# Loads of the delta-rule chain in a function of their own, issued two tiles ahead into three buffers

## The chip, the cores and the metric

The kernel runs on 1 core of one Trainium2 chip. The metric is the time of one execution on the device in microseconds (us), taken as the median of several runs. The core's engines each work through a queue of their own, in order: TensorE (PE, matmuls), VectorE (DVE), ScalarE (ACT), GpSimd (POOL) and SyncE (SP), which here issues nearly all DMA transfers.

## The reference

Two layers (DEPTH = 2) of a hybrid block on 2048 latent tokens and a prefix of 256 context tokens. Each layer projects the normalised input once and feeds three groups of heads, whose outputs are concatenated and projected back: a bidirectional state-space scan (SSD), a bidirectional gated delta rule (GDN), and attention over all 2304 tokens. The change concerns the delta rule. Per direction, head and chunk of 64 tokens it computes

```python
def step(S, inp):
    qd, kd, u_i, w_i, a_i, d_i = inp
    v_new = u_i - jnp.einsum('bhcd,bhde->bhce', w_i, S)
    o = jnp.einsum('bhcd,bhde->bhce', qd, S) + jnp.einsum('bhij,bhje->bhie', a_i, v_new)
    S = S * d_i[..., None, None] + jnp.einsum('bhcd,bhce->bhde', kd, v_new)
    return S, o
```

so each chunk needs the state S that the chunk before it leaves.

## The kernel before

The tokens are 18 tiles of 128 (NT = 18, 2 of context and 16 latent). In each layer the kernel projects the input, prepares the delta rule (`gdn_pre`, `gdn_solve`, which store per tile what the chain needs in DRAM), runs the SSD, and then the delta-rule chain (`gdn_chain`) beside attention; at the end comes the output projection (line 1231).

Attention is written as a generator. Eight of its 24 large units stand before the chain in the code, the others behind it. A planner of the framework turns the code into one queue per engine ahead of time: it gives an instruction a place when it expects its inputs to be there and its buffers to be free, by its own estimates of durations, and prefers what stands earlier in the code. So attention's matmuls (lines 531, 562, 563, 556) fill PE between those of the chain, and with them come attention's maxima (`mx`, line 533, and `nm`, line 535) and the low halves `pl` (line 571) on VectorE and the exponentials on ScalarE. Once planned, the queues run in that order on the chip.

In the chain, tile u stands for tile u of the forward direction and tile rev(u) of the backward one, side by side. Three functions work on it, all in pool `gw` with two buffers per name, and `slot` gives them banks of one PSUM pool of four; buffers and banks of a pool are handed out in the order of the code.

- `prep(u)` (line 1036) issues 13 DMA loads on SP's queue: `acv` (3 pieces by `by_chunk`, so its rows carry line 1034), `xf` (4, line 1050), `xt_` (2, line 1052), `kq` (2, line 1054, shown as `kqc`) and `er` (2, line 1055). Then it computes: `kq` times `er` in place (line 1056 on VectorE for k, line 1060 on GpSimd for q), `kdw` (line 1058, GpSimd), the mask on `acv` in place (line 1061, VectorE), and the off-diagonal block of the inverse by two rounds of small matmuls (lines 1067 and 1076) with copies on ScalarE. After it `er` and `xt_` are no longer needed; `kq`, `acv` and `xf` are read on by the step.
- `step(u)` does two chunks (s = 0, 1), each a chain of k S (line 1100), r (line 1104, VectorE), the inverse times r (line 1114), V (line 1119, ScalarE), the update (line 1123; the output at lines 1109 and 1125) and the new S (`Sc`, line 1127, VectorE).
- `out(u)` normalises and gates the output of the tile, in the second half of the tiles.

The loop calls prep(u + 1), then step(u), then out(u - 1). The tiles `xf` are kept by hand in a list of two, `xf[u % 2]`, as parts of them stay zero.

Of the kernel before, what the change touches and what calls it, by code (L numbers as in the profile page):

```python
# [9 lines left out]
F32 = mybir.dt.float32  # L10
# [7 lines left out]
P = 128  # L18
# [4 lines left out]
NT = NTOK // P  # L23
# [14 lines left out]
def rev(t):  # L38
    return TC - 1 - t if t < TC else NT + TC - 1 - t
# [45 lines left out]
def hybrid_kernel(ctx, tc, x, c, ctx_in, c_ctx, norm_w, w_mod, b_mod, w_in, conv_w, conv_b, ssd_A_log,  # L85
# [158 lines left out]
    for l in range(DEPTH):  # L244
# [246 lines left out]
        with ExitStack() as bx:  # L491
# [13 lines left out]
            def slot(name):  # L505
                return psg[1].tile([P, 512], F32, name=name, tag="g")
# [108 lines left out]
            def next_layer():  # L615
                if not last:
                    Ln.append(layer_tiles())
                    layer_vectors(l + 1, Ln[0], ps=sslot)
                    yield
                    yield from modulation(l + 1, Ln[0], ps=sslot, wmp=wmp)  # L620
                    layer_rows(l + 1, Ln[0])
# [59 lines left out]
            ot0 = TC if last else 0  # L681
# [324 lines left out]
            def gdn_chain(rq):  # L1006
# [6 lines left out]
                with ExitStack() as gx:  # L1013
                    gr = gx.enter_context(tc.tile_pool(reuse_waits="tile", name="gr2", bufs=1))
                    gw = gx.enter_context(tc.tile_pool(reuse_waits="tile", name="gw2", bufs=2))
                    xf = [gr.tile([P, 2, 4, 64], F32, name=f"xf{i}") for i in range(2)]
                    for i in range(2):
                        nc.gpsimd.memset(xf[i], 0.0)
                    S = gw.tile([P, 4, 64], F32, name="Sc")
                    nc.gpsimd.memset(S, 0.0)  # L1020
# [8 lines left out]
                    def by_chunk(d, dram2, tile3, store=False):  # L1029
                        v = dram2.rearrange("(c p) x -> p c x", c=2)  # L1030
                        for i in ((slice(0, 2),) if d == 0 else (0, 1)):
                            j = i if d == 0 else 1 - i
                            a, b_ = tile3[tk[d], i], v[:, j]
                            nc.sync.dma_start(b_, a) if store else nc.sync.dma_start(a, b_)

                    def prep(u):
                        tl = (u, rev(u))
                        want_o = u >= ot0
                        xu = xf[u % 2]
                        xt = gw.tile([P, 2, 4, 32], F32, name="xt_")  # L1040
                        kq = gw.tile([P, 2, 4, P], F32, name="kqc")
                        er = gw.tile([P, 4, P], F32, name="er")
                        acv = gw.tile([P, 2, 4, 4, 64], F32, name="acv")
                        k0 = 0 if want_o else 1
                        for d in range(2):
                            td = tl[d]
                            tsl = slice(td * P, (td + 1) * P)
                            by_chunk(d, pre_d[td, :, k0:4].rearrange("p k h n -> p (k h n)"), acv[:, :, k0:4].rearrange("p c k h n -> p c (k h n)"))
                            for a, bb, cx in ((d, b0, c0), (1 - d, b1, c1)):
                                nc.sync.dma_start(xu[bb[d], :, :, cx[d]].rearrange("p c h i -> p (c h) i"),  # L1050
                                                  xd_d[d, 0, td, a].rearrange("c h j i -> j (c h) i"))
                            nc.sync.dma_start(xt[b0[d]].rearrange("p c h i -> p (c h) i"), xd_d[d, 1, td, d].rearrange("c h j i -> j (c h) i"))
                            nk = 2 if want_o else 1
                            nc.sync.dma_start(kq[dk[d], 0:nk].rearrange("p k h n -> p (k h) n"), kt_d[0:nk * 256, tsl].rearrange("(h p) n -> p h n", p=64))
                            nc.sync.dma_start(er[dk[d]], eg_d[d:d + 1, :, u].to_broadcast([64, 4, P]))
                        nc.vector.tensor_tensor(out=kq[:, 0], in0=kq[:, 0], in1=er, op=ALU.mult)
                        kdw = gw.tile([P, 2, 4, 64], F32, name="kdw")
                        nc.gpsimd.tensor_tensor(out=kdw, in0=acv[:, :, 3], in1=kdc[:, u, :, :, None].to_broadcast([P, 2, 4, 64]), op=ALU.mult)
                        if want_o:
                            nc.gpsimd.tensor_tensor(out=kq[:, 1], in0=kq[:, 1], in1=er, op=ALU.mult)  # L1060
                            nc.vector.tensor_tensor(out=acv[:, :, 0], in0=acv[:, :, 0], in1=msk[:, None, None, :].to_broadcast([P, 2, 4, 64]), op=ALU.mult)
                        pv = slot("pv")
                        pvv = pv[:, 0:256].rearrange("p (c h n) -> p c h n", c=2, h=4)
                        for c in range(2):
                            for h in range(4):
                                for d in range(2):
                                    nc.tensor.matmul(pvv[b1[d], c, h, :], acv[b0[d], 1 - c if d else c, 1, h, c1[d]], xt[b0[d], c, h, :],
                                                     start=True, stop=True, tile_position=(b0[d].start, b1[d].start))
                        vt = gw.tile([P, 2, 4, 32], F32, name="vt")
                        for d in range(2):  # L1070
                            nc.scalar.activation(out=vt[b1[d]], in_=pvv[b1[d]], func=AF.Copy, scale=-1.0)
                        pzv = pv[:, 256:512].rearrange("p (c h n) -> p c h n", c=2, h=4)
                        for c in range(2):
                            for h in range(4):
                                for d in range(2):
                                    nc.tensor.matmul(pzv[b0[d], c, h, :], vt[b1[d], c, h, :], xu[b1[d], c, h, c1[d]],
                                                     start=True, stop=True, tile_position=(b1[d].start, b0[d].start))
                        for d in range(2):
                            nc.scalar.copy(out=xu[b0[d], :, :, c1[d]], in_=pzv[b0[d]])
                        return xu, kq, acv, kdw  # L1080
# [84 lines left out]
                                nc.sync.dma_start(mx_d[384:640, n0:n0 + 64].rearrange("(m p) n -> p m n", p=P), mt[:, c, :, tk[d]])  # L1165

                    pend = None
                    nxt = prep(0)
                    for u in range(NT):
                        cur, nxt = nxt, prep(u + 1) if u + 1 < NT else None  # L1170
                        S, ox = step(u, S, *cur)
                        if pend is not None:
                            out(*pend)
                        pend = (u, *ox) if ox is not None else None
# [14 lines left out]
            for _ in range(8):  # L1189
                next(att)  # L1190
            banks(0, 4)
            gdn_chain(rq)
            for _ in att:
                pass
# [55 lines left out]
            pend, ahead = [], next_layer()  # L1250
# [53 lines left out]
```

## Time and profile before

| what | value |
|---|---|
| median of 3 runs | 4039.15 us (4035.92 to 4040.36) |
| the profiled execution | 4035.59 us |
| its span | 4033.8 us |
| mean granted clock of PE | 0.969 |
| PE busy | 3776.4 us (94%) |
| VectorE busy | 2720.7 us (67%) |
| ScalarE busy | 1800.4 us (45%) |
| GpSimd busy | 1351.1 us (33%) |

The profile is of one execution; times inside it are counted from the start of its span. A row of a wait names who waited, for whom, the us in total, how often, and the longest. In a timeline row the bracket at the end is the idle time of the engine just before the instruction, and what ended it. PE's clock is given as the granted share of full speed: 1.00 is 2.4 GHz and 0.50 is 1.2 GHz, and a value between them is a mean over a stretch.

### The profile page before, as it was taken

What the parts mean: (1) busy time and instruction counts of PE and PEld (TensorE: products, weight loads), DVE (VectorE), ACT (ScalarE), POOL (GpSimd) and SP (SyncE); (2) the same over time, 40 slices, a digit from 0 to 9 for tenths busy, and PEclk for the clock granted to TensorE, in tenths of its full rate; (3) what the DMA queues carried; (4) which work ended last, traced back from release to release, by engine and by line L of the source; (5) the groups of instructions that cost most, each with busy time, mean ns of one, the idle gap of its engine ahead of it and who ended that gap; (6) DMA issues with size and microseconds to landing.
All of it is one profiled execution on the core that took longest, in us unless ns stands there. A gap on an engine that the chain in (4) does not pass through costs nothing. (4 is left out here: it accounts for less than half of the span.)

```text
span 4033.8 us, 70483 instructions
## 1 busy us (share of the span) xinstructions
PE 3776.4 (94%) x25750; PEld 2839.4 (70%) x25750; DVE 2720.7 (67%) x5372; ACT 1800.4 (45%) x3728; POOL 1351.1 (33%) x1760
## 2 busy tenths in 40 slices
PE   7999999999999888897999999999898999888989
PEld 5899999554566556565678999996554665556667
DVE  6556573789977567774547574746888776667733
ACT  5343332443466455564214443423333655556610
POOL 5112130477476221321213030303774662123100
PEclk9999999999999889998999999999999999989999
DMA  6343432345222544535744433332452215444344
GB/s 202 98 144 112 133 105 95 104 151 173 69 60 60 111 105 103 116 73 181 241 153 130 152 111 130 118 100 77 144 175 72 61 55 118 101 104 120 85 140 154
DMA packets 549798, 477.72 MB, mean 118 GB/s; under 512 B 133128, under 2 KB 487372, under 8 KB 549452
## 3 DMA queue, kind: packets, MB, share of 16 engines
q1 hardware_dynamic: 507596, 437.82, 37.1%
q10 hardware_dynamic: 41856, 35.40, 2.9%
q8 instruction: 203, 3.33, 0.3%
q14 instruction: 143, 1.17, 0.1%
HBM read 328.91 MB, written 144.18 MB: 117 GB/s over the span
## 5 line engine op out<-in xcount | busy, mean ns | idle before, releaser
L565 ACT ACTIVATE pe<-pst 128x512 f32<-128x512 f32 (+1 forms) x876 | 511.8, 594 | 692.0 <-PE pst L563 654.3
L533 DVE TENSOR_REDUCE mx<-pq 128x1 f32<-128x512 f32 (+1 forms) x972 | 590.6, 626 | 131.1 <-PE pq L531 127.0
L531 PE MATMUL pq<-khh,q 128*128 128x512 f32 (+1 forms) x972 | 459.9, 498 | 38.7 <-DVE mx L533 32.1
L556 PE MATMUL po<-pe,v 128*65 128x512 f32 x960 | 488.5, 597 | 0.8 <-ACT os__11676 L579 0.8
L562 PE MATMUL pst<-q,khh 128*128 128x512 f32 (+1 forms) x876 | 429.3, 490 | 16.8 <-DVE mx L533 14.0
L455 PE MATMUL ps<-lo,wh 128*128 128x384 f32 (+2 forms) x1296 | 441.3, 340 | 0.0
L455 PE MATMUL ps<-hi,wl 128*128 128x384 f32 (+2 forms) x1296 | 441.0, 340 | 0.0
L455 PE MATMUL ps<-hi,wh 128*128 128x384 f32 (+2 forms) x1296 | 440.9, 340 | 0.0
L571 DVE TENSOR_TENSOR pl<-pe,ph 128x512 fp32r<-128x512 f32 x396 | 309.6, 786 | 118.6 <-ACT ph L570 54.3
L563 PE MATMUL pst<-qm,klo 65*128 65x512 f32 (+1 forms) x876 | 356.9, 408 | 0.0
L401 PE MATMUL ps<-wh,hi 128*128 128x320 f32 (+1 forms) x1120 | 354.4, 318 | 0.1
L401 PE MATMUL ps<-wl,hi 128*128 128x320 f32 (+1 forms) x1120 | 350.8, 314 | 0.0
L401 PE MATMUL ps<-wh,lo 128*128 128x320 f32 (+1 forms) x1120 | 350.2, 315 | 0.5 <-DVE lo L366 0.5
L531 PEld LDWEIGHTS pq<-khh,q 128*128 128x128 f32 x972 | 186.7, 195 | 190.2 <-DVE mx L533 73.6
L570 ACT CAST ph<-pe 128x512 fp32r<-128x512 f32 x396 | 243.8, 620 | 94.0 <-PE po L556 36.4
L376 DVE TENSOR_TENSOR wl<-wt,wh 128x1024 fp32r<-128x1024 f32 (+3 forms) x144 | 175.3, 1246 | 160.2 <-ACT wh L375 159.8
L556 PE MATMUL po<-ph,vh 128*65 128x512 f32 x792 | 262.2, 413 | 7.7 <-ACT os__20088 L579 4.6
L562 PEld LDWEIGHTS pst<-q,khh 128*128 128x128 f32 x876 | 171.3, 196 | 128.7 <-issue 53.5
L455 PEld LDWEIGHTS ps<-lo,wh 128*128 128x128 f32 x1296 | 244.0, 188 | 10.8 <-issue 0.4
L455 PEld LDWEIGHTS ps<-hi,wh 128*128 128x128 f32 x1296 | 243.5, 188 | 10.3
L455 PEld LDWEIGHTS ps<-hi,wl 128*128 128x128 f32 x1296 | 243.4, 188 | 10.3
L1231 PE MATMUL psd<-woh,mh 128*128 128x512 f32 x544 | 218.7, 402 | 19.0 <-ACT mh L1222 17.6
(588 smaller groups left out, 8136.4 us busy)
## 6 DMA issues: line engine op xcount, KB each, us to landing
wt<-in_w_in_dram SPq DMA_DIRECT2D x72, 512.0 KB
wmt<-in_w_mod_dram SPq DMA_DIRECT2D x48, 512.0 KB
pre_d<-pre SPq DMA_DIRECT2D x34, 512.0 KB
acv<-pre_d SPq DMA_DIRECT2D x34, 512.0 KB
kqc<-kt_d SPq DMA_DIRECT2D x68, 256.0 KB
acv<-pre_d SPq DMA_DIRECT2D x68, 256.0 KB
wt<-in_w_in_dram SPq DMA_DIRECT2D x24, 668.0 KB
wt<-in_w_in_dram SPq DMA_DIRECT2D x24, 640.0 KB
```

What stands on the lines that cost most here:

```text
L376: nc.vector.tensor_tensor(out=wl[:, ks, :], in0=wt, in1=wh[:, ks, :].bitcast(F32), op=ALU.subtract)
L401: nc.tensor.matmul(ps, hh[:, k, a], ww[:, k, :], start=(n == 0), stop=(n == 3 * KD - 1))
L455: nc.tensor.matmul(ps, ww[:, k, m * P:(m + 1) * P], hh[:, k, s0:s0 + sn], start=(n == 0), stop=(n == 3 * KD - 1))
L531: nc.tensor.matmul(pq[:, :n], q2[:, u * P:(u + 1) * P], khh[:, kvh, k0t * P + a:k0t * P + a + n], start=True, stop=True)
L533: nc.vector.tensor_reduce(mx[:, i:i + 1], pq[:, :n], axis=AX.X, op=ALU.max)
L556: nc.tensor.matmul(po[0:65, :qn], v[:, kt, vs], p[:, :qn], start=(kt == k0t and j == 0), stop=(kt == k1t - 1 and j == len(ops) - 1))
L562: nc.tensor.matmul(pt[:, :qn], khh[:, kvh, ks], q2[:, :qn], start=True, stop=False)
L563: nc.tensor.matmul(pt[:, :qn], klo[:, kvh, ks], qm[:, :qn], start=False, stop=True)
L565: nc.scalar.activation(out=pe[:, :qn], in_=pt[:, :qn], func=AF.Exp, scale=0.125)
L570: nc.scalar.copy(out=ph, in_=pe)
L571: nc.vector.tensor_tensor(out=pl, in0=pe, in1=ph.bitcast(F32), op=ALU.subtract)
L1231: nc.tensor.matmul(ps, a, w[k][:, n * 512:n * 512 + 512], start=(k == 0 and i == 0), stop=(k == KD - 1 and i == 2))
```

## The change

`prep` is split. A function `load(u)` allocates the five tiles and issues the 13 loads; `prep` takes the tiles and only computes. The five tiles get three buffers in place of two: `xf` becomes a list of three with `xf[u % 3]`, the others get `bufs=3`. The loop issues load(0) and load(1) before prep(0), and load(u + 2) ahead of prep(u + 1). The transfers, the arithmetic, `step` and `out` stay.

```diff
-                    xf = [gr.tile([P, 2, 4, 64], F32, name=f"xf{i}") for i in range(2)]
-                    for i in range(2):
+                    xf = [gr.tile([P, 2, 4, 64], F32, name=f"xf{i}") for i in range(3)]
+                    for i in range(3):
                         nc.gpsimd.memset(xf[i], 0.0)
...
-                    def prep(u):
+                    def load(u):
                         tl = (u, rev(u))
                         want_o = u >= ot0
-                        xu = xf[u % 2]
-                        xt = gw.tile([P, 2, 4, 32], F32, name="xt_")
-                        kq = gw.tile([P, 2, 4, P], F32, name="kqc")
-                        er = gw.tile([P, 4, P], F32, name="er")
-                        acv = gw.tile([P, 2, 4, 4, 64], F32, name="acv")
+                        xu = xf[u % 3]
+                        xt = gw.tile([P, 2, 4, 32], F32, name="xt_", bufs=3)
+                        kq = gw.tile([P, 2, 4, P], F32, name="kqc", bufs=3)
+                        er = gw.tile([P, 4, P], F32, name="er", bufs=3)
+                        acv = gw.tile([P, 2, 4, 4, 64], F32, name="acv", bufs=3)
                         k0 = 0 if want_o else 1
...
                             nc.sync.dma_start(er[dk[d]], eg_d[d:d + 1, :, u].to_broadcast([64, 4, P]))
+                        return u, xu, xt, kq, er, acv
+
+                    def prep(u, xu, xt, kq, er, acv):
+                        want_o = u >= ot0
                         nc.vector.tensor_tensor(out=kq[:, 0], in0=kq[:, 0], in1=er, op=ALU.mult)
...
                     pend = None
-                    nxt = prep(0)
+                    ahead = [load(0), load(1)]
+                    nxt = prep(*ahead.pop(0))
                     for u in range(NT):
-                        cur, nxt = nxt, prep(u + 1) if u + 1 < NT else None
+                        if u + 2 < NT:
+                            ahead.append(load(u + 2))
+                        cur, nxt = nxt, prep(*ahead.pop(0)) if ahead else None
                         S, ox = step(u, S, *cur)
```

## Rows read from the trace of the kernel before

**Rows 1.** The page's first part: busy us, share of the span, instructions.

```profile
PE 3776.4 (94%) x25750; PEld 2839.4 (70%) x25750; DVE 2720.7 (67%) x5372; ACT 1800.4 (45%) x3728; POOL 1351.1 (33%) x1760
```

**Rows 2.** Table by stages: the stretches with the chain, layers 0 and 1.

```profile
core 0: us, PE busy (x) PEld busy (x) DVE busy (x) ACT busy (x) POOL busy (x), PEclk, DMA share, GB/s
...
1326.00:1822.00 496.00, 435.02 (x5307) 293.65 (x5306) 343.21 (x617) 290.58 (x557) 119.86 (x109) 0.91 0.46 105
...
3336.00:3808.00 472.00, 420.62 (x5161) 283.00 (x5160) 335.89 (x606) 285.76 (x545) 115.14 (x102) 0.94 0.45 108
```

**Rows 3.** The same table: the chain's end in layer 1, after its last loads.

```profile
3755.00:3790.00 35.00, 34.90 (x357) 23.34 (x353) 29.82 (x61) 25.96 (x48) 8.98 (x7) 1.00 0.14 36
```

**Rows 4.** Waits of PE in the two stretches, layer 0, then layer 1.

```profile
engine line waited for: us in total, times, longest us
PE pv L1067 <- DMA acv<-pre_d: 22.6, 9, 4.8
PE po L556 <- DVE pl L571: 8.3, 6, 3.1
...
PE pq L531 <- DVE nm L535: 2.5, 1, 2.5
PE pv L1067 <- DMA xt__12789<-xd_d: 1.2, 1, 1.2
...
PE pv L1067 <- DMA acv<-pre_d: 23.7, 10, 5.0
PE pq L531 <- DVE mx L533: 6.3, 4, 2.2
...
PE p L1100 <- DVE Sc L1127: 0.8, 1, 0.8
...
PE pv L1067 <- DMA xt__33913<-xd_d: 0.3, 1, 0.3
```

**Rows 5.** Timeline of VectorE: one tile, and S before the last step.

```profile
start us, us, engine line op out<-in xcount [idle before <-releaser]
3510.38 0.41 DVE L1127 TENSOR_TENSOR Sc<-sd,p 128x256 f32<-128x256 f32 x1
...
3514.56 0.69 DVE L1056 TENSOR_TENSOR kqc<-kqc,er 128x512 f32<-128x512 f32 x1 [2.27 <-DMA kqc<-kt_d]
...
3772.33 0.41 DVE L1127 TENSOR_TENSOR Sc<-sd,p 128x256 f32<-128x256 f32 x1
```

**Rows 6.** Timeline of PE at the same places.

```profile
3517.30 0.22 PE L1067 MATMUL pv<-xt__35007,acv 32*32 32x32 f32 x2 [3.56 <-DMA acv<-pre_d]
3517.45 0.68 PE L1100 MATMUL p<-Sc,kqc 64*64 64x64 f32 x16
...
3772.80 0.68 PE L1100 MATMUL p<-Sc,kqc 64*64 64x64 f32 x16
```

**Rows 7.** Timeline of SP's queue in the same tile: DMA issues.

```profile
3507.67 0.61 SPq L1054 DMA_DIRECT2D kqc<-kt_d  x1
...
3511.18 1.15 SPq L1034 DMA_DIRECT2D acv<-pre_d  x1
...
3516.40 1.26 SPq L1055 DMA_DIRECT2D er<-eg_d  x2
3523.04 0.80 SPq L1052 DMA_DIRECT2D xt__35343<-xd_d  x2
```

**Rows 8.** View of tile Sc: count, duration, first and last start of line 1127.

```profile
L1127 DVE TENSOR_TENSOR Sc<-sd,p x72: 404/418/424, 1357.7 to 3779.9; 128x256 f32<-128x256 f32 x72
```

**Rows 9.** What line 1056 waited for (us, times); then line 1061, layer 0.

```profile
  DMA kqc<-kt_d: 66.7, 26
...
  DMA er<-eg_d: 1.9, 3
...
DVE acv L1061 <- DMA acv<-pre_d: 6.3, 4, 2.2
```

**Rows 10.** Timeline of a tile where VectorE alone stopped PE.

```profile
3415.37 0.69 DVE L1056 TENSOR_TENSOR kqc<-kqc,er 128x512 f32<-128x512 f32 x1 [2.09 <-DMA kqc<-kt_d]
...
3417.79 0.45 PE L556 MATMUL po<-pl,vh 128*65 128x512 f32 x1 [3.02 <-DVE pl L571]
```

**Rows 11.** Table by stages, 5 us each, at and after the wait.

```profile
3515.00:3520.00 5.00, 2.70 (x28) 2.23 (x29) 5.00 (x9) 0.62 (x1) 1.37 (x1) 0.88 0.93 235
3520.00:3525.00 5.00, 5.00 (x70) 2.88 (x69) 2.16 (x5) 3.32 (x7) 1.21 (x1) 0.78 0.10 18
```

## Prediction

> **What bounds the kernel now.** I read the page first: TensorE (PE) is busy 94% of a span of 4033.8 us [rows 1], so a gain has to come out of the 6% in which it is idle, or out of time in which it is busy at the lower clock. The table by stages says where that is. In the two stretches that hold the delta-rule chain (1326 to 1822 us in layer 0, 3336 to 3808 us in layer 1) PE is busy 435.0 of 496 us and 420.6 of 472 us, with a mean granted clock of 0.91 and 0.94 [rows 2]. That is 61.0 + 51.4 = 112.4 us idle. What PE ran below full pace I take as busy time x (1 - clock): 435.0 x 0.09 + 420.6 x 0.06 = 39 + 25 = 64 us. Where the chain's last loads have landed (3755 to 3790 us), PE is busy 34.90 of 35 us at clock 1.00 [rows 3], so attention can fill PE around the chain.
>
> Next the waits of PE in these stretches [rows 4]. Line 1067, the first matmuls of the preparation, waited 38.5 us in layer 0 (five rows, the first and last shown) and 34.0 us in layer 1 (six rows), mostly for the load of `acv`: 72.5 us. Waits for VectorE (DVE) take 17.7 us (four rows, 10 waits) and 13.2 us (four rows, 9 waits): 30.9 us in 19 waits, 1.6 us each. The other 9.0 us belong to ScalarE at the stage's end and to gaps too short for the view.
>
> One tile in detail. The state S is done at 3510.38 + 0.41 = 3510.8 us [rows 5]. Next on PE's queue stands line 1067, which waits 3.56 us for `acv`, until 3517.30; line 1100, which needs S and nothing of `acv` but takes its PSUM bank after line 1067's, runs right behind it at 3517.45, 6.7 us after its input was there [rows 6]. In the last step, where no preparation is pending, line 1100 follows S by 3772.80 - 3772.74 = 0.06 us [rows 5, 6]. So the load stands in the chain and, PE's queue being in order, in front of attention too. SP's queue says why: the loads of `kq` and `acv` go out at 3507.67 and 3511.18, as the step that used their buffers ends, while `er` and `xt_`, whose buffers come free inside the preparation, go out at 3516.40 and 3523.04 for the tile after the next [rows 7]. The order of the code does not hold the loads back; two buffers do.
>
> **The change, part by part.** It adds no transfer: the 13 DMA issues of a tile stay, on SP's queue. It adds one memset of `xf` per layer (on GpSimd, ahead of the chain, beside attention: nothing) and 17 KiB per partition (`xf` 2, `xt_` 1, `kq` 4, `er` 2, `acv` 8). The larger pool may reach into the space where w_out is staged and hold that back until the chain ends; the last S comes at 3779.9 us [rows 8], 28 us before the stretch ends at 3808, and will come earlier, so I cost it at nothing; without this cover I would put it at the size of the 9 us that stand at the stage's end now.
>
> *Line 1067.* Tile u+2's loads go out when step u-1 ends and are used a whole step later. A tile takes up to 26 us (472 us over 18 tiles [rows 2]); `acv` landed 6.1 us after its issue (3511.18 to 3517.30) [rows 6, 7]. 26 against 6 leaves no wait: the 72.5 us go, but for some 5 us of the first tile. What SP is moved past are the partial-sum loads and stores and attention's q loads; they are used a step later and have slack. Banks are handed out in the order of the code, so `pv` of tile u+1 gets its bank after the last of step u-1; it is then ready, and I take no new wait there (bounds: none, or the 0.68 us of line 1100's matmuls a tile [rows 6]).
>
> *What is late next: VectorE.* Line 1056 multiplies `kq` in place by `er`. It needs no new buffer, so nothing holds it until its turn: the planner will put it into VectorE's queue where it expects `kq` to have landed, now in the middle of the step before. On the chip `kq` lands later than that: 2.27 us idle in this tile [rows 5], 79.2 us over the kernel (four rows, 33 waits), 2.2 us a tile [rows 9]. Everything on VectorE waits behind it, attention's `pl` and `mx`, and then PE. In the tile at 3415 us this alone stopped PE for 3.02 us, with VectorE idle 2.09 us [rows 10]. Today this wait mostly lies under that of line 1067 and costs little of its own; the cover goes. The bounds are 0 (the chain's own matmuls, which are no longer late, fill PE) and 36 x 3.02 = 109 us; I take the mean of the waits for VectorE that are seen, 36 x 1.6 = 58 us, since PE gets about 1 us of chain work to run meanwhile.
>
> Here a rule of the Trainium skill speaks against the change (DMA: Bandwidth & Descriptors, Rules for kernel authors): to hide a DMA, issue it early and wait for it late. The early issue is what the diff does; line 1056 still waits early (2.27 us [rows 5]), so by this rule the time would be that of the second rival, 4015 us, and not the sum below.
>
> *The clock.* After this wait the granted clock is 0.78 over 3520 to 3525 us [rows 11]: part of the time at the 1.2 GHz level. I let the 64 us shrink with the idle time (bounds 0 and 64).
>
> **The sum**, against the profiled execution's 4035.6 us (its span 4033.8; the median of the three runs is 3.5 us higher, inside their spread): idle 72.5 + 30.9 - 58 = 45 us; clock 64 x 45 / 103.4 = 28 us. 4035.6 - 73 = 3963 us. The chain itself becomes shorter by more (about 5 us a tile, 90 us a layer), but its end does not set the time: attention's matmuls behind it do, and they are all still there.
>
> **Rivals.** *Both waits vanish.* For it: the chain's end at 99.7% busy [rows 3], and that line 1056 gets a whole step of slack if the planner leaves it next to line 1067. Against: nothing in the code makes it wait for that. 103 us idle and most of the 64 us of clock go: 4036 - 156 = 3880 us (3870 to 3915). The Trainium skill's reading of a repeated gap as too few buffers (Perfetto Trace Analysis, Optimization Strategy) gives this outcome; the tile at 3415 us, stopped by VectorE alone, shows that buffers are not all of it.
>
> *The wait only moves.* Line 1056 stops PE for 2.2 us a tile, VectorE's full wait, or more: 36 x 2.2 = 79 us stay of 103, 24 us idle and 64 x 24 / 103 = 15 us of clock are saved, 3996 us; at 2.9 us a tile (103.4 / 36, today's mean) nothing is saved. 3996 to 4036, I say 4015 us. For it: rows 10. The case in which the third buffers bring no load forward lies at its upper end.
>
> *Slower: two waits on VectorE.* `acv` lands 2.7 us after `kq` is usable (3517.30 against 3514.56). If line 1061, the mask on `acv`, is put at its expected landing too, VectorE waits a second time, 2.7 - 0.7 (line 1056's work) = 2.0 us. So far that wait is small (6.3 us in 4 waits in layer 0 [rows 9]), as PE's stop delays what stands in front of it. Then 36 x (2.2 + 2.0) = 151 us idle against 103, and 64 x 48 / 103 = 30 us more of clock: up to 4114 us, I say 4080. It decides from the point where PE loses more than 2.9 us a tile. Against: the planner's distance from line 1056 to 1061 covers most of it today.
>
> **How the numbers follow.** Forecast (3930 to 3996) 0.47, both vanish 0.18, only moved 0.22, slower 0.13. The range 3890 to 4045 leaves out half of the first rival and most of the last, 2 in 10. A measurement can tell 0.2%, 8 us, from no change. Faster by more than that: 0.47 + 0.18 + 0.14 of the second rival = 0.79; the same: its other 0.08 and 0.01 of the last; slower 0.12.
>
> **What will show it.** Right: line 1067 no longer among PE's long waits for `acv`; line 1100 follows S within 3 us in every step (6.7 us in the tile above); the last S (now 3779.9 us [rows 8]) comes some 100 us or more earlier; PE's rest is ended by `pl`, `mx` and `nm`, with line 1056 still waiting some 2 us a tile for `kq`. Wrong, towards 3880: line 1056 without a wait and clock 1.00 throughout. Wrong, upwards: line 1067 still waits, or lines 1056 and 1061 wait over 3 us together and PE with them.

## The result, and the profile after

The changed kernel takes 4000.9 us in the median of four runs (3989.3 to 4007.4), the kernel before 4037.9 us beside it: a ratio of 0.9905, with a 95% interval of 0.9876 to 0.9933. Run again later beside other kernels it took 3998.4 us (3996.0 to 4000.7), ratio 0.9918 (0.9894 to 0.9943). So it is faster by 37 us, 0.9%. The forecast was 3963 us. Direction and range held; half of the gain did not come.

The profiled execution after took 3989.3 us, 46.3 us less than the one before, where the sum had 73. The first part of its page:

```profile
span 3987.5 us, 70354 instructions
...
PE 3758.9 (94%) x25750; PEld 2817.7 (71%) x25750; DVE 2704.5 (68%) x5372; ACT 1799.1 (45%) x3728; POOL 1347.3 (34%) x1762
```

Against [rows 1] PE's busy time fell by 17.5 us and its idle time from 257.4 to 228.6 us (span less busy), by 28.8 us. Both terms of the sum moved, both by less than forecast (28 and 45).

The table by stages, from some 20 us ahead of the chain's first matmul to its last S, layers 0 and 1 (columns: stretch, its length, busy us of each engine with instruction counts, clock granted to PE, DMA share, GB/s):

```profile
1331.00:1731.00 400.00, 357.70 (x5040) 236.05 (x5038) 273.35 (x513) 237.73 (x465) 116.92 (x105) 0.96 0.55 124
3307.00:3693.00 386.00, 353.53 (x4903) 233.82 (x4902) 269.50 (x505) 232.47 (x455) 108.27 (x99) 0.97 0.52 122
```

PE is idle for 42.3 + 32.5 = 74.8 us, and busy time x (1 - clock) is 14.3 + 10.6 = 24.9 us. Before, in stretches cut in the same way, these were 102.7 and 60.8 us (112.4 and 64 in the somewhat longer stretches of [rows 2]):

```profile
1326.00:1792.00 466.00, 410.55 (x5204) 277.80 (x5203) 319.24 (x577) 264.96 (x515) 115.89 (x106) 0.91 0.48 107
3336.00:3780.00 444.00, 396.72 (x5060) 268.06 (x5059) 312.19 (x564) 262.57 (x508) 111.17 (x99) 0.94 0.45 108
```

The clocks are rounded to 0.01, so a sum of two such products is known to some 4 us.

What PE waited for there, layer 0 and then layer 1:

```profile
PE po L556 <- DVE pl L571: 17.8, 13, 4.5
PE pq L531 <- DVE mx L533: 8.2, 6, 1.9
PE p L1118 <- DVE r L1108: 4.6, 5, 2.0
...
PE pv L1071 <- DMA xt__12791<-xd_d: 1.9, 1, 1.9
PE pv L1071 <- DMA xt__12808<-xd_d: 1.6, 1, 1.6
...
PE po L556 <- DVE pl L571: 11.3, 11, 2.0
PE pq L531 <- DVE mx L533: 8.4, 8, 2.0
...
PE pv L1071 <- DMA xt__33876<-xd_d: 0.6, 1, 0.6
```

Line 1071 is line 1067 of before. Its 72.5 us [rows 4] are down to 4.1 us, in the first tiles of each layer. Now nearly all that PE waits for is VectorE (68.4 us with the rows not shown). And VectorE waits for the loads, at two places (line 1060 is the multiply of `kq` by `er`, line 1056 before; line 1065 the mask on `acv`, line 1061 before); the largest rows over the whole kernel:

```profile
DVE kqc L1060 <- DMA kqc<-kt_d: 76.9, 29, 4.6
DVE acv L1065 <- DMA acv<-pre_d: 31.8, 17, 4.2
DVE acv L1065 <- issue: 13.3, 7, 3.1
DVE acv L1065 <- DMA er<-eg_d: 10.5, 5, 2.7
DVE kqc L1060 <- DMA er<-eg_d: 5.7, 3, 2.6
```

With the smaller rows line 1060 waits 83.5 us (79.4 before) and line 1065 waits 61.2 us. What line 1061, the mask, waited for before, 17.8 us in all:

```profile
  DMA acv<-pre_d: 10.5, 8
  issue: 5.2, 5
  DMA zzg<-zn_d: 2.1, 1
```

The view infers which transfer ended a wait. The mask reads no `er`, so an `er` in front of line 1065 has to be read as a late transfer of the tile's load, by the code one of `acv`. One tile shows how. SP's queue, VectorE and PE:

```profile
1500.88 0.61 SPq L1054 DMA_DIRECT2D kqc<-kt_d  x1
1504.41 0.59 SPq L1054 DMA_DIRECT2D kqc<-kt_d  x1
1505.12 0.58 SPq L1034 DMA_DIRECT2D acv<-pre_d  x1
1507.09 1.25 SPq L1034 DMA_DIRECT2D acv<-pre_d  x2
...
1504.38 0.41 DVE L1131 TENSOR_TENSOR Sc<-sd,p 128x256 f32<-128x256 f32 x1
1508.32 0.69 DVE L1060 TENSOR_TENSOR kqc<-kqc,er 128x512 f32<-128x512 f32 x1 [2.75 <-DMA kqc<-kt_d]
1510.62 0.41 DVE L1108 TENSOR_TENSOR r<-acv,p 128x256 f32<-128x256 f32 x1
1514.34 0.69 DVE L1065 TENSOR_TENSOR acv<-acv,msk 128x512 f32<-128x512 f32 x1 [2.19 <-DMA er<-eg_d]
...
1506.40 0.68 PE L1104 MATMUL p<-Sc,kqc 64*64 64x64 f32 x16
1509.66 0.50 PE L531 MATMUL pq<-khh,q 128*128 128x512 f32 x1 [1.05 <-DVE mx L533]
1515.69 0.44 PE L556 MATMUL po<-pl,vh 128*65 128x512 f32 x1 [2.29 <-DVE pl L571]
```

S is done at 1504.79 us and line 1104 (1100 before) follows it at 1506.40, not 6.7 us later as in [rows 5, 6]. But the loads issued from 1500.88 us on, which a step will need only a whole step later, are read by VectorE at once: line 1060 stands 2.75 us, until the transfer issued at 1504.41 has landed, and line 1065 another 2.19 us. PE's first products of that tile stand at 1525.71 us. Attention's `mx` and `pl` stand behind them on VectorE, and PE behind those: 1.05 us, then 2.29 us.

### The profile page after: what moved, and what is told of

Its sections match the earlier page's. It is cut to its first block, busy times and chain, and to the rows that moved or that the text cites. A ratio compares the mean times of both kernels' runs of the same rounds, so it can differ in the third digit from the quotient of the medians.

```text
span 3987.5 us, 70354 instructions
## 1 busy us (share of the span) xinstructions
PE 3758.9 (94%) x25750; PEld 2817.7 (71%) x25750; DVE 2704.5 (68%) x5372; ACT 1799.1 (45%) x3728; POOL 1347.3 (34%) x1762
## 5 line engine op out<-in xcount | busy, mean ns | idle before, releaser
L571 DVE TENSOR_TENSOR pl<-pe,ph 128x512 fp32r<-128x512 f32 x396 | 296.7, 755 | 72.3 <-ACT ph L570 38.2
L455 PEld LDWEIGHTS ps<-hi,wh 128*128 128x128 f32 x1296 | 243.5, 188 | 10.3
L1238 PE MATMUL psd<-woh,mh 128*128 128x512 f32 x544 | 220.9, 406 | 18.1 <-ACT mh L1229 16.6
```

The lines of the kernel that those rows point to most:

```text
L455: nc.tensor.matmul(ps, ww[:, k, m * P:(m + 1) * P], hh[:, k, s0:s0 + sn], start=(n == 0), stop=(n == 3 * KD - 1))
L571: nc.vector.tensor_tensor(out=pl, in0=pe, in1=ph.bitcast(F32), op=ALU.subtract)
L1238: nc.tensor.matmul(ps, a, w[k][:, n * 512:n * 512 + 512], start=(k == 0 and i == 0), stop=(k == KD - 1 and i == 2))
```

## The experiments

The theory after the first reading: the third buffers took the load wait off PE's queue. What they left is on VectorE's, where the two multiplies are placed by the planner about where it expects the load to have landed, and not where their result is needed. The main rivals: these waits are slack; they are the price of too few buffers; the two waits are one. Line numbers shift by a few between the kernels, so the text names the operation; "first products" are the first matmuls of the preparation, line 1067 before. `behind(a, b)`, which the kernel before has already, tells the planner to place `a` after `b`. Every edit lets the planner order the queues anew, so a difference of some us need not be the edit's own.

All stretches in the table are cut as above. "Idle" and "clock" are PE's idle us and busy x (1 - clock) in both chain stages; the next columns are idle us, short gaps included, of VectorE in front of the `kq` and mask multiplies and of PE in front of the first products of the preparation. The ratio is to the kernel before on the same chip.

| kernel | median us | ratio to before (95%) | idle | clock | kq | mask | first products |
|---|---|---|---|---|---|---|---|
| before | 4037.9 | 1 | 102.7 | 60.8 | 79.4 | 17.8 | 72.7 |
| changed | 4000.9 | 0.9905 (0.9876 to 0.9933) | 74.8 | 24.9 | 83.5 | 61.2 | 4.2 |
| changed, again | 3998.4 | 0.9918 (0.9894 to 0.9943) | 73.3 | 32.2 | 82.5 | 60.8 | 4.2 |
| both multiplies held back | 3905.4 | 0.9677 (0.9655 to 0.9698) | 20.3 | 6.8 | 4.7 | 4.8 | 5.0 |
| `kq` multiply held back | 4010.7 | 0.9936 (0.9917 to 0.9955) | 78.4 | 54.9 | 5.5 | 111.6 | 2.5 |
| mask held back | 3963.5 | 0.9821 (0.9800 to 0.9842) | 53.0 | 32.3 | 78.5 | 3.2 | 2.8 |
| three buffers, old code order | 3996.9 | 0.9901 (0.9880 to 0.9922) | 74.0 | 40.1 | 85.6 | 57.4 | 2.5 |
| before, both multiplies later | 4016.1 | 0.9953 (0.9938 to 0.9969) | 83.7 | 58.3 | 1.1 | 2.7 | 82.9 |
| two buffers, all readers later | 3960.6 | 0.9817 (0.9792 to 0.9842) | 49.6 | 40.7 | 1.7 | 9.8 | 34.5 |
| four buffers | 3997.1 | 0.9912 (0.9883 to 0.9941) | 73.9 | 40.0 | 83.4 | 60.0 | 3.8 |
| third buffer for `acv`, `xt_`, `xf` only | 3982.8 | 0.9874 (0.9850 to 0.9899) | 72.8 | 36.6 | 77.2 | 53.5 | 5.7 |
| the same, multiplies later | 3932.9 | 0.9758 (0.9728 to 0.9788) | 39.2 | 21.2 | 0.4 | 2.4 | 5.0 |

### Both multiplies held back

```
+ mm = nc.vector.tensor_tensor(out=kq[:, 0], in0=kq[:, 0], in1=er, op=ALU.mult)
+ if last:
+     behind(mm, last[-1])
...
+     mm = nc.vector.tensor_tensor(out=acv[:, :, 0], in0=acv[:, :, 0], in1=msk[:, None, None, :].to_broadcast([P, 2, 4, 64]), op=ALU.mult)
+     if last:
+         behind(mm, last[-1])
...
+ last.append(nc.vector.tensor_tensor(out=Sn, in0=sd, in1=pc, op=ALU.add))
```

> The changed kernel with one thing more: the two VectorE multiplies of the preparation (kqc by er, acv by msk) may not start before the previous step's last state update on VectorE, so they run one whole step after their loads were issued. Theory (VectorE's load waits): in the changed kernel VectorE stands 83.5 us at the kqc multiply and 61.2 us at the acv multiply for loads, and of TensorE's 74.8 us of idle time in the two chain stages nearly all is behind VectorE. Held back, both waits go to under 10 us, TensorE's idle time in the two stages falls to 20 to 35 us, part of the 25.5 us of low-clock loss goes too: 3950 us (3925 to 3975) against 4001. Rival 1 (the waits are only slack that VectorE would have anyway, the chain's own dependences set the idle): the waits go, the idle stays near 75 us, 4000 us (3985 to 4010). Rival 2 (the two multiplies, 1.4 us a tile, now stand between the state update and the next residual and delay it): the waits go but each of 36 tiles pays 1.4 us on the chain, 50 us lost against 50 won, 4000 us, with the residual line waiting for VectorE and not for TensorE.

Measured: 3905.4 us, 95 us under the changed kernel. The table by stages and the waits of VectorE:

```profile
1329.00:1685.00 356.00, 342.03 (x5030) 231.00 (x5029) 284.39 (x512) 234.68 (x460) 119.08 (x105) 0.99 0.63 138
3263.00:3609.00 346.00, 339.67 (x4904) 231.24 (x4903) 278.13 (x505) 231.85 (x456) 110.75 (x99) 0.99 0.59 136
```

```profile
DVE kqc L1060 <- DMA er<-eg_d: 4.7, 3, 2.4
DVE acv L1067 <- issue: 2.8, 1, 2.8
DVE acv L1067 <- DMA acv<-pre_d: 2.0, 1, 2.0
```

PE is idle 14.0 + 6.3 = 20.3 us in place of 74.8, and the clock is 0.99. Both rivals fall: the waits were not slack, and the multiplies' work in their new place does not set the chain (no row of PE is left that waits for `r`; in the changed kernel there are 7.2 us of them). The gain is larger than expected, 3905 against 3925 to 3975 us; the sum of idle and clock fell by 54.5 + 18.1 = 73 us, and the time by 95 us (the profiled executions: 3902.2 against 3989.3 us, 87 us). By the two pages the 87 us are 57.2 us of idle time and 29.9 us of busy time; some 12 us of the busy time lie outside of the chain stages, and why is open. This is the fastest kernel of the study: the changed one's work, with two ordering rules more. Its page:

```profile
PE 3729.0 (96%) x25750; PEld 2807.1 (72%) x25750; DVE 2726.2 (70%) x5372; ACT 1797.1 (46%) x3728; POOL 1350.5 (35%) x1762
```

### One of the two alone

Each of these keeps one half of the diff above.

> Only the kqc multiply is held back, the acv multiply stays where the changed kernel has it. Theory: the wait of 83.5 us at the kqc multiply goes, that at the acv multiply (61.2 us) stays; gaps of TensorE near kqc's wait were 48.9 us in sum: 3970 us (3950 to 3990), about half of what holding both gives. Rival (what one wait leaves the other takes, since both wait for the transfers of the same load): the acv multiply then waits more than 61 us, and the time stays at 3990 to 4005.

> Only the acv multiply is held back, the kqc multiply stays. Theory: the wait of 61.2 us at the acv multiply goes, the 83.5 us at kqc stay; gaps of TensorE near acv's wait were 51.4 us in sum: 3970 us (3950 to 3990). If the acv wait alone is what the change newly cost (17.8 us before, 61.2 after), this gives about 25 us. Rival (the waits are slack): 3990 to 4005.

Holding back the `kq` multiply alone won nothing (4010.7 us, a little above the rival's 4005): the rival was right. What that wait leaves, the mask takes, as both read transfers of the same load and `acv` lands last. The largest rows of VectorE in that kernel (line 1067 is the mask):

```profile
DVE acv L1067 <- DMA acv<-pre_d: 54.3, 16, 4.6
DVE acv L1067 <- DMA er<-eg_d: 35.5, 8, 5.7
DVE acv L1067 <- issue: 7.0, 3, 3.2
```

With the smaller rows the mask waits 111.6 us, against 61.2 in the changed kernel. Holding back the mask alone gave 3963.5 us, inside the range expected: PE is idle for 53.0 us. So the mask's wait, which the change had raised from 17.8 to 61.2 us, costs 35 to 37 us, as long as the `kq` wait stands. 10 us lost and 37 us won alone and 95 us won together do not add up; the two waits are in part one wait. The forecasts' 48.9 and 51.4 us of gaps could not tell them apart: together they are more than the 74.8 us of idle time, so they hold some gaps twice.

### The buffers without the code order

```
- xu = xf[u % 2]
+ xu = xf[u % 3]
- kq = gw.tile([P, 2, 4, P], F32, name="kqc")
+ kq = gw.tile([P, 2, 4, P], F32, name="kqc", bufs=3)
...
  def prep(u):
      tl = (u, rev(u))
```

> The kernel before with the third buffers alone: the loads stay inside the preparation, one tile ahead in the program's text. Theory (buffers do it, since each queue is ordered at build time by when work is ready, and a free buffer lets the loads be issued a step earlier wherever they stand in the text): the same as the changed kernel, 4001 us (3985 to 4015), TensorE's wait at the first products of the preparation under 10 us. Rival (the loads have to stand ahead of the preparation in the text): near the kernel before, 4038 us (4025 to 4045), with TensorE's wait there near 72 us.

3996.9 us, with all columns of the table near the changed kernel's but the clock's: the buffers do it, the move of the loads in the text does nothing that can be measured.

### The multiplies later, with two buffers

```
+ def late(prev):
+     mm = nc.vector.tensor_tensor(out=kq[:, 0], in0=kq[:, 0], in1=er, op=ALU.mult)
+     if prev is not None:
+         behind(mm, prev)
...
- nc.vector.tensor_tensor(out=Sn, in0=sd, in1=pc, op=ALU.add)
+ add = nc.vector.tensor_tensor(out=Sn, in0=sd, in1=pc, op=ALU.add)
+ if s == 0 and mid is not None:
+     mid(add)
```

`mid` is the next tile's `late`, which holds the mask multiply too.

> The kernel before, two buffers and loads one tile ahead, with the two VectorE multiplies alone moved: they may not start before the state update of the first half of the running step. TensorE's first products of the preparation stay where they were, so their wait for the loads (72.5 us) stays. Theory (the two waits are two separate prices): VectorE's 97 us of load waits go, the 30.9 us that TensorE stood behind VectorE go, and some of the clock loss: 4000 us (3980 to 4020) against 4037. Rival (the two waits overlap, TensorE stops at its own wait for the same load instead): its wait at the first products grows and the time stays at 4025 to 4045.

4016.1 us: VectorE's waits went from 97.2 to 3.8 us and PE's idle time by 19.0 us, not the full 30.9 of [rows 4], since PE's own wait for the loads grew by 10 us. Its main rows (line 1073 is the first products here):

```profile
PE pv L1073 <- DMA acv<-pre_d: 50.0, 24, 4.1
PE pv L1073 <- issue: 19.8, 7, 3.9
PE pv L1073 <- DMA o_d<-ox: 9.5, 3, 4.4
```

Theory and rival each hold in part. From here to both multiplies held back with the third buffers is another 111 us: the two steps are worth more together than the 19 and 37 us that each gives alone to the kernel before.

### All readers later, with two buffers

```
+ if s == 0 and ld is not None:
+     nx = prep(*ld, add, mm)
```

The whole preparation comes after the first half step, the multiplies behind `add`, the first products behind `mm`, the last matmul of the half step.

> Two buffers and loads one tile ahead as before, but everything that reads the loads on VectorE and TensorE stands behind the first half of the running step: the two multiplies behind its state update, the first products of the preparation behind its last matmul. Theory (what counts is the time between issue and use on the waiting queues, not the number of buffers): near the version with three buffers and both multiplies held back, 3905 us; as half a step is only about 10 us and the loads take longer in some tiles, 3920 us (3900 to 3945). Rival (half a step is too short without the third buffer): waits of over 50 us come back at the multiplies or the first products, 3960 to 4010 us.

3960.6 us, at the edge of the rival, with 46 us of load waits in all, a little under its 50: half a step is too short for `acv`. What is left of PE's wait at the first products is nearly all one row:

```profile
PE pv L1075 <- DMA acv<-pre_d: 30.5, 21, 2.7
```

That two buffers and three ordering rules beat the three buffers of the change (3960.6 against 4000.9 us) fits the theory that the time between issue and use counts, on each queue that waits. That 3905 us is not reached fits what the third buffer is for, a whole step of lead for the first products; the 29 us of idle time between the two kernels (49.6 and 20.3) are about the 29.5 us that the first products wait longer (34.5 and 5.0).

### Four buffers

```
- ahead = [load(0), load(1)]
+ ahead = [load(0), load(1), load(2)]
...
- kq = gw.tile([P, 2, 4, P], F32, name="kqc", bufs=3)
+ kq = gw.tile([P, 2, 4, P], F32, name="kqc", bufs=4)
...
- acv = gw.tile([P, 2, 4, 4, 64], F32, name="acv", bufs=3)
+ acv = gw.tile([P, 2, 4, 4, 64], F32, name="acv", bufs=4)
```

> The changed kernel with four buffers of xf, xt_, kqc and acv and the loads three tiles ahead; nothing is held back. Theory (the two multiplies stand on VectorE where the scheduler expects the landing, so that however early the load, they follow it): VectorE's load waits stay over 100 us, the time stays at 4000 us (3980 to 4015). Rival (a transfer that is issued a step earlier still has landed by then): the waits go, 3905 to 3950 us.

`er` keeps three. 3997.1 us, the two waits 83.4 and 60.0 us: an earlier load is followed by its multiplies. Counted from 0, VectorE multiplies the `kq` of tile 10 in step 7 of layer 0 (at 1514.67 us), where the changed kernel multiplies that of tile 9 (at 1508.32 us). The lead that the buffers give goes to nobody on VectorE.

### The third buffer where PE reads it

```
- xu = xf[u % 2]
+ xu = xf[u % 3]
- xt = gw.tile([P, 2, 4, 32], F32, name="xt_")
+ xt = gw.tile([P, 2, 4, 32], F32, name="xt_", bufs=3)
...
- acv = gw.tile([P, 2, 4, 4, 64], F32, name="acv")
+ acv = gw.tile([P, 2, 4, 4, 64], F32, name="acv", bufs=3)
```

> The kernel before with a third buffer for acv, xt_ and xf alone, what TensorE's first products read; kqc and er keep two. Theory (the gain of the change is the end of TensorE's wait at these products): the wait of 72.5 us falls under 10 us, the time is that of the changed kernel, 4000 us (3980 to 4020). Rival (the buffers of kqc and er carry the gain, or the load queue holds acv back behind kqc): 4025 to 4045 us.

3982.8 us: all of the gain comes from the third buffer of `acv`, `xt_` and `xf`. It is even some 14 us less than with four buffers of nearly everything, measured beside it; why was not looked into.

### The same, with the multiplies later

The edits of the last kernel and of the one with the multiplies later and two buffers, together.

> The kernel before with the third buffer for acv, xt_ and xf alone (as in the run that gave 3983 us), and the two VectorE multiplies behind the state update of the first half of the running step; kqc and er keep two buffers. Theory (lead in time on each queue that waits: a step for TensorE's first products, half a step for the two multiplies, which waited 1.1 and 2.7 us in all when held there with two buffers): the three waits go, 3905 us (3895 to 3925), as with three buffers of everything. Rival (with TensorE no longer stopping, half a step shrinks to some 9 us and the loads of kqc and er come too late for it, so the multiplies wait again): 3930 to 3980 us, with over 40 us of VectorE's load waits.

3932.9 us: neither. All three load waits are gone (0.4, 2.4 and 5.0 us), as the theory had it, and yet it is 28 us slower than with both multiplies held back for a whole step. PE's idle time is 39.2 us against 20.3. One row that the faster kernel doesn't have stands for 10.3 us of it:

```profile
PE p L1129 <- ACT Vc L1125: 10.3, 8, 2.1
```

In eight places PE stands at the products of V until ScalarE has delivered it. The planner made another order of the whole stage; what in it costs the rest stays open.

### The changed kernel again

> The changed kernel once more, beside the others on one chip, since its runs scattered by 18 us: 3997 us (3985 to 4010), between the two versions that give nearly the same order of work (3997 us both). A result under 3985 or over 4015 would mean that the gain measured first was off.

3998.4 us, as expected: the first result was not an accident of its runs.

## Why the prediction was right, and half right

*Line 1067.* Right. Its 72.5 us went to 4.1 us, the 5 us that I had left for the first tiles. Line 1100 follows S within 3.3 us in every step (forecast 3; two steps are over it). The run with the third buffers of `acv`, `xt_` and `xf` alone shows that this step carries the whole gain.

*What is late next.* Right about the engine, the line and the cause; the `kq` multiply waits 83.5 us, 2.3 us a tile, as read from [rows 9]. Wrong about the number of waits. The sum took one wait on VectorE, at 58 us of PE's idle time. There were two, and PE is idle for 74.8 - 4.1 = 70.7 us. The mask's wait stood among the rivals, with the argument against it that the planner's distance from line 1056 to 1061 covers most of it. That was the step that failed: the cover was not the distance but PE's stop at line 1067. In nearly all tiles of both kernels the mask stands behind the first `r` on VectorE's queue. As long as that `r` came late, since line 1100 stood behind line 1067, most of `acv`'s landing lay under it, as in the tile of [rows 5], where the mask does not wait:

```profile
3518.64 0.41 DVE L1104 TENSOR_TENSOR r<-acv,p 128x256 f32<-128x256 f32 x1
...
3519.93 0.69 DVE L1061 TENSOR_TENSOR acv<-acv,msk 128x512 f32<-128x512 f32 x1
```

In the median of the tiles with `r` between the two multiplies (31 before, 28 after), `r` starts 4.1 us after the `kq` multiply before and 2.3 us after it in the changed kernel; the mask's turn, when all in front of it is done, comes after 5.6 and 3.9 us, and it starts after 6.0 and 5.6 us. So the landing hardly moved, and the turn came 1.7 us earlier. The change removed the stop and with it the cover: in every kernel of the table in which the first products no longer wait and the mask is not held back, the mask waits 53 us or more. The sign that I had named for "wrong, upwards", both waits over 3 us together, came: 144.7 / 36 = 4.0 us a tile. That the rival's waits were nearly exact, 151 us forecast and 144.7 measured, is partly luck: it had `acv` landing 2.7 us after `kq` and the mask's turn 0.7 us after it, and both come some 3 us later. Its price was wrong. I let each of these us stop PE for one, and all that PE lost but for the first products was 70.7 us, about half. So the time was not slower.

The run with the mask held back is the case that the sum described, one wait on VectorE at line 1056. It took 3963.5 us against the forecast 3963, with 53.0 us idle (58 in the sum) and 32.3 us of clock (64 - 28 = 36 in the sum). That the times agree to 1 us is luck: against the kernel before, its profiled execution has 56.1 us less idle time (45 in the sum) and 16.3 us less busy time (28).

*The clock.* The term was under-sized where it was read. I let 64 us shrink by 28; in the chain stages they shrank to 24.9 and 32.2 us in the two executions of the changed kernel. It scatters: five executions with 72.8 to 74.8 us of idle time in the table show 24.9 to 40.1 us of it. But PE's busy time as a whole fell only by 17.5 us in one execution, where the clock in the chain stages alone gave back 60.8 - 24.9 = 35.9 us. Part of the difference lies in the last stretch, behind attention, at 0.94:

```profile
3803.00:3987.00 184.00, 163.49 (x664) 129.07 (x663) 67.21 (x108) 15.99 (x28) 16.20 (x16) 0.94 0.49 159
```

The stretch with the same work before (3852 to 4033 us) had 0.97, with PE busy for 158.86 us; in the second execution of the changed kernel it had 0.96, so this part scatters too.

*The sum.* Of its 73 us, 45 were idle time and 28 the clock. The profiled execution gained 46.3 us: 28.8 us of idle time and 17.5 us of busy time. Outside of the chain stages the idle time is the same in both kernels (257.4 - 102.7 = 154.7 and 228.6 - 74.8 = 153.8 us). So the 16 us that the idle term lacks lie in the chain, where the run with the mask held back puts the mask's wait at 74.8 - 53.0 = 21.8 us. What else did not reach the end is busy time outside of the chain stages, some 18 us; 5 us of it are in the last stretch just shown, and the rest stays open. The miss of 38 us in the median is thus 16 us of idle time, 10 us of busy time and 12 us by which the median of the changed kernel lies above its profiled execution.

*What I costed at nothing.* No new wait for a bank shows at line 1071, and w_out's split comes earlier than before (1753.8 to 1769 us in layer 0; 1814 to 1825 before). The chain, from line 1104's first matmul to its last S, became 66 and 59 us shorter, not 90 a layer: its last S stands at 3692.6 us, 87 us earlier and not 100 or more.

*The rivals.* "Both waits vanish" did not happen, and was put at 3880 us with the remark that nothing in the code makes line 1056 wait for its turn. The run that adds just that took 3905.4 us. "The wait only moves" has the right time (3996 to 4036), though the wait at line 1056 stops PE for less than the full wait that it assumed.

*The rule on when to wait.* By the Trainium skill's rule (DMA: Bandwidth & Descriptors, Rules for kernel authors) of issuing early and waiting late, as the prediction read it, the time was to be 4015 us, and 4000.9 was measured; the trace agrees with the rule, with the wait of 2.75 us above, and the runs give the worth of its second half as 95 us. The reading of a repeated gap as too few buffers (the Trainium skill, Perfetto Trace Analysis, Optimization Strategy) holds for the third buffer of `acv`; a fourth left the 74 us of idle time as they were.

## What to carry to other kernels

A third buffer moves a load earlier, but every instruction that reads it in place moves with it if a planner places it by when its input should have landed: look at each engine that reads the load, and tie the readers that nobody needs yet to a later instruction of their own queue. Before a wait is costed, ask which other wait makes it look small: a wait that goes uncovers what stood behind it (17.8 us became 61.2 here). And a wait on an engine beside the bound is worth a fraction of its length: with both multiplies held back, 135 us of VectorE's waits went (144.7 to 9.5), and PE's idle time in the chain stages fell by 54.5 us and the time by 95 us.

## What was not expected of the hardware

The same multiply on VectorE takes longer where an instruction of GpSimd is already under way. In the changed kernel line 1060 takes 693 ns in the median, held back it takes 1202 ns, and the mask 1097 ns. Durations (min/median/max) with both held back:

```profile
L1060 DVE TENSOR_TENSOR kqc<-kqc,er x36: 679/1202/1280, 1345.8 to 3574.6; 128x512 f32<-128x512 f32 x36
...
L1067 DVE TENSOR_TENSOR acv<-acv,msk x34: 685/1097/1101, 1343.3 to 3575.8; 128x512 f32<-128x512 f32 x34
```

The timeline of one tile with both held back, GpSimd and VectorE:

```profile
1492.45 0.61 POOL L1110 TENSOR_TENSOR sd<-Sc,dsc 128x256 f32<-128x256 f32 x1 [3.57 <-DVE Sc L1135]
1499.21 1.04 POOL L1064 TENSOR_TENSOR kdw<-acv,kdc 128x512 f32<-128x512 f32 x1 [6.14 <-PE p L1133]
1500.21 1.06 POOL L1110 TENSOR_TENSOR sd<-Sc,dsc 128x256 f32<-128x256 f32 x1
...
1499.57 1.23 DVE L1060 TENSOR_TENSOR kqc<-kqc,er 128x512 f32<-128x512 f32 x1
1500.72 1.10 DVE L1067 TENSOR_TENSOR acv<-acv,msk 128x512 f32<-128x512 f32 x1
```

GpSimd's `kdw` was under way when the first multiply began, and each of the two multiplies took some 0.4 to 0.5 us longer; `sd` on GpSimd took 1.06 us and not 0.61 (its duration at 1492 us). The Trainium skill (SBUF — State Buffer, SBUF: two separate sides) says that a VectorE instruction with two SBUF inputs and a GpSimd instruction that reads SBUF share a pair of ports that one of them holds for its whole length while the other stands still; this tile agrees with that to 0.14 us (1500.25, the end of `kdw`, plus 0.69 is 1500.94 us, seen 1500.80). What counts is who starts first: of the 36 `kq` multiplies held back, 30 start with GpSimd under way and take 1.20 us in the median, the other six 0.69. In the changed kernel GpSimd's own multiply of `kq` starts just behind VectorE's in 32 of 36 tiles; there VectorE takes 0.69 us, and GpSimd's takes 1.78 us in the median, against 1.32 with both held back. In the tile at 1508.32 us:

```profile
1508.36 1.78 POOL L1064 TENSOR_TENSOR kqc<-kqc,er 128x512 f32<-128x512 f32 x1 [2.42 <-DMA kqc<-kt_d]
```

VectorE's busy time rose by 21.7 us over the changed kernel's, and the fastest kernel pays that. Whether another place for the two multiplies would save it was not tried.
